# Layer 0's feed-forward gate vector summed on VectorE, GpSimd and ScalarE during the latent heads, and the third head pair's split one step a job

## The chip, the cores and the metric

The kernel runs on one core of a Trainium2 chip. A core has TensorE (matrix products, called PE in the profile; its weight loads are PEld), VectorE (DVE), ScalarE (ACT), GpSimd (POOL) and SyncE (SP, which here only issues DMAs). Each engine executes its own instructions in order and waits for the others by semaphores. The metric is the device time of one execution in microseconds (us), the median of several runs.

## What is computed

Two transformer layers over 512 latent tokens and 256 context tokens, 1024 features, all in float32. Each layer is modulated by six vectors per stream, made from a conditioning vector; the sixth, `g_f`, is the gate of the feed-forward part. Cut to what matters:

```python
for l in range(DEPTH):
    sh_a, sc_a, g_a, sh_f, sc_f, g_f = jnp.split(silu_c @ mod_w[l] + mod_b[l], 6, axis=-1)
    csh_a, csc_a, cg_a, csh_f, csc_f, cg_f = jnp.split(silu_cc @ mod_w[l] + mod_b[l], 6, axis=-1)
    a_lat, a_ctx = modulate(h_lat, sh_a, sc_a), modulate(h_ctx, csh_a, csc_a)
    ...                          # l = 0: latent heads and 2-D neighbourhood heads; l = 1: sliding window heads
    h_lat = h_lat + g_a * o_lat
    h_lat = h_lat + g_f * swiglu(modulate(h_lat, sh_f, sc_f), ffn_w_gate_up[l], ffn_w_down[l])
    if l == 0:                   # the same for the context stream, with csh_a ... cg_f
        ...
return rms_norm(h_lat, final_norm)
```

## The kernel before

The activations lie transposed, features on the 128 partitions and tokens along the free dimension, in eight tiles of 128 features. Products of full precision are made of three products of split operands: a value is cast to a high part on ScalarE and the rest is subtracted on VectorE (`split`, `parts`, `load_w`). A planner orders the instructions of each engine: it simulates the engines with its own costs and takes, of what is ready, what the program emitted first. `shifted(n)` makes what is emitted under it n places less urgent. Some stretches of the feed-forward part have a fixed order on TensorE.

Layer 0 runs in these stages, with the times of the profiled execution:

- To about 185: the input projections (`projections`, 94 steps).
- About 185 to 263: the neighbourhood heads, four pairs of heads, `na_jobs`. A pair is three jobs: the context queries, then the queries of blocks 0 and 1, then of 2 and 3. A job makes scores on TensorE, row maxima on VectorE (`take`, L546, the bias added), exponentials on ScalarE (`exps`, L542), transposes on TensorE (L483), their copies to SBUF on VectorE and ScalarE (L474, L475) and weighted sums on TensorE (L536). `attend` runs the front half of one job beside the back half of the job ahead of it, in the order of the letters of `PATTERN` (f for the front, b for the back, s for one step of side work).
- About 263 to 400: the latent heads, eight heads of two jobs, `mla_jobs`, built in the same way. Two heads ahead, `latent_operands` splits operands on ScalarE and GpSimd and copies rows by DMA on the SP queue.
- About 400 to 465: the output projection. Then the feed-forward part, `ffn`, 22 columns of 128: the first directly (`first_pairs`), the others as `Pair`s.

Side work comes from two sources. Generators that are put in the queue by `beside` advance by `step`; the number of steps a job is `STEPS`, for the four pairs of the neighbourhood heads `STEPS[0]`. One of them is `split_pair(p)`, which splits the queries (first step) and the keys (second step) of the third and fourth pair; the engine of the keys' high cast is chosen by `RK` (0: ScalarE, 2: VectorE), at L744, and the rest is subtracted on VectorE at L735.

The other source is `all_mods`, which makes the modulation vectors in the order of their need, one unit for each `next`: for layer 0 the components 2, 4, 3, 5, then those of layer 1. `bg(n)` takes n units. A component named in `PE_MODS` is made by `mods_pe`, four units: a unit loads four tiles of 256 KB on the SP queue, multiplies them on TensorE against `cond_col` (L191, 16 instructions in four column groups of 32), copies the result on ScalarE (L193), sums the groups by four small products with `pick` (L195) and adds the bias on VectorE (L199). Any other component of layer 0 is made by `mod_tile` from rows of `mod_w`, eight tiles of 512 KB in two halves, two units a tile. The first unit loads both halves and sums their products with the latent stream's conditioning vector on VectorE (L241, L245). The second multiplies the halves by the context stream's vector on GpSimd (L258), sums them on ScalarE (L259) and adds the two sums and the bias on VectorE (L261, L262). So components 2 and 3 are 16 units each, and 4 and 5, in `PE_MODS`, 4 each. Layer 1's tiles are loaded by GpSimd's queue (L212) into the tags rope0 and nb and summed on VectorE alone (L219).

In the projections `bg` takes 0.43 units a step from the ninth step on, 37 in all: components 2, 4 and 3 (36 units) and the first unit of component 5. In the heads it takes none, since the rates `BG[0]` are 0. In the feed-forward part the pairs 1 and 2 take two units each: the other three units of component 5 and the first tile of layer 1. Component 5 is used for the first time by `down0`, behind the fourth column.

## Time and profile before

| | us |
|---|---|
| median of 3 runs | 1573.08 |
| lowest and highest run | 1572.73 and 1574.07 |
| the profiled execution | 1573.01 |
| its span, from the first to the last instruction | 1571.2 |
| TensorE busy in the span | 1524.4 |
| VectorE busy | 1180.6 |
| ScalarE busy | 804.4 |
| GpSimd busy | 282.3 |
| mean granted TensorE clock | 0.992 |

Times within the execution are us from the start of the span. A row of the timeline gives start, length, engine, line, operation and operands, with the idle time ahead of it and what ended it in brackets. A row of the waits gives who waited for whom, the total in us and the number of times. Matmuls are pipelined, so that a matmul's length in the timeline is more than its share of TensorE's time; the distance from one start to the next, or the chain of waits, gives that share.

### The profile page before, as it was taken

How to read it: one execution, taken by the hardware profiler on the slowest of the kernel's cores; microseconds unless marked ns; L12 is line 12 of the kernel's file. 1: busy time of each engine (PE TensorE's matmuls, PEld its weight loads, DVE VectorE, ACT ScalarE, POOL GpSimd, SP SyncE). 2: the span in 40 equal slices, each digit the busy share in tenths (PEclk: the TensorE clock that was granted, in tenths of full speed). 3: DMA queues.
4: the chain of work that ended last, by engine and by line, in shares of the span. 5: the costliest groups of instructions: out<-in, count | busy, mean ns of one | idle time of the engine just before them, and what ended most of it. 6: DMA issues, size and time to landing. Idle time of an engine off the chain costs nothing.

```text
span 1571.2 us, 26600 instructions
## 1 busy us (share of the span) xinstructions
PE 1524.4 (97%) x9942; PEld 1355.7 (86%) x9942; DVE 1180.6 (75%) x2351; ACT 804.4 (51%) x1638; POOL 282.3 (18%) x316
## 2 busy tenths in 40 slices
PE   6999889999999999999999999999999999999998
PEld 4787767887998999999999999877789998899997
DVE  5494878657588588895877776888877778688686
ACT  5354587777376234242433345557866445354453
POOL 0173724233010010111112110382002000000000
PEclk9999999999999999999999999999999999999999
DMA  9457242102462465656566665130016133233232
GB/s 343 153 170 235 77 132 76 44 11 95 164 224 88 148 207 174 224 156 241 179 214 245 205 242 194 40 117 32 1 29 187 45 103 130 89 100 124 86 101 88
DMA packets 82129, 216.63 MB, mean 138 GB/s; under 512 B 10832, under 2 KB 18896, under 8 KB 82000
## 3 DMA queue, kind: packets, MB, share of 16 engines
q1 hardware_dynamic: 66640, 163.02, 32.4%
q0 software_dynamic: 13056, 48.77, 9.1%
q10 hardware_dynamic: 2304, 3.15, 0.5%
q8 instruction: 78, 1.28, 0.3%
q14 instruction: 51, 0.42, 0.1%
HBM read 187.10 MB, written 23.07 MB: 134 GB/s over the span
## 4 chain that ended last, share of the span: by engine, by line
PE 74%; DVE 6%; issue 4%; DMA 3%; ACT 2%; POOL 0%; DVEq 0%; POOLq 0%; ACTq 0%; SPq 0%
PE pso L536 5%; PE pss L1408 4%; PE pss L1406 4%; PE pss L1407 4%; PE pss L324 3%; PE pss L325 3%; PE psd L324 3%; PE pss L326 3%; PE psd L1408 3%; PE psd L325 3%; PE psd L1406 3%; PE psd L326 3%; PE psd L1407 3%; PE pss L768 3%; PE pst L483 2%
## 5 line engine op out<-in xcount | busy, mean ns | idle before, releaser
L311 ACT CAST wh<-wr 128x512 fp32r<-128x512 f32 (+2 forms) x139 | 105.9, 776 | 197.4 <-DMA wr<-in_w_dn_dram 39.9
L312 DVE TENSOR_TENSOR wl<-wr,wh 128x512 fp32r<-128x512 f32 (+2 forms) x136 | 127.5, 944 | 71.2 <-ACT wh L311 70.6
L542 ACT ACTIVATE p<-p,sm 128x512 f32<-128x512 f32 (+3 forms) x144 | 105.1, 730 | 34.0 <-DVE sm L546 33.3
L1408 PE MATMUL pss<-b,wl 128*128 128x384 f32 (+1 forms) x302 | 93.8, 311 | 1.9 <-DVE wl L1394 1.9
L1406 PE MATMUL pss<-b,wh 128*128 128x384 f32 (+1 forms) x302 | 93.6, 310 | 0.0
L1407 PE MATMUL pss<-b,wh 128*128 128x384 f32 (+1 forms) x302 | 93.5, 310 | 0.0
L536 PE MATMUL pso<-ph,b 128*64 128x256 f32 (+1 forms) x400 | 78.3, 354 | 2.3 <-DVE ph L474 2.1
L1406 PE MATMUL psd<-b,wh 128*128 128x384 f32 (+1 forms) x256 | 79.8, 312 | 0.6 <-ACT p L1456 0.6
L1407 PE MATMUL psd<-b,wh 128*128 128x384 f32 (+1 forms) x256 | 79.8, 312 | 0.0
L1408 PE MATMUL psd<-b,wl 128*128 128x384 f32 (+1 forms) x256 | 79.2, 311 | 0.0
L325 PE MATMUL psd<-b,wh 128*128 128x512 f32 (+3 forms) x224 | 78.4, 350 | 0.0
L536 PE MATMUL pso<-pl,b 128*64 128x256 f32 (+1 forms) x400 | 77.7, 353 | 0.2 <-ACT pl L475 0.2
L768 PE MATMUL pss<-st,st 128*128 128x512 f32 (+2 forms) x264 | 69.8, 379 | 7.8 <-DVE sm L546 7.6
L324 PE MATMUL pss<-st,wh 128*128 128x256 f32 (+2 forms) x226 | 75.5, 334 | 0.6 <-ACT st L1393 0.6
L326 PE MATMUL pss<-st,wl 128*128 128x256 f32 (+2 forms) x226 | 75.4, 334 | 0.0
L324 PE MATMUL psd<-b,wh 128*128 128x512 f32 (+3 forms) x208 | 74.9, 360 | 0.1
L326 PE MATMUL psd<-b,wl 128*128 128x512 f32 (+3 forms) x208 | 73.4, 354 | 0.0
L325 PE MATMUL pss<-b,wh 128*128 128x256 f32 (+3 forms) x223 | 70.5, 318 | 0.0
L1393 ACT CAST wh<-ph 128x512 fp32r<-128x512 f32 x80 | 46.4, 620 | 33.4 <-DVE ph L1428 14.3
L1393 ACT CAST wh<-pl 128x512 fp32r<-128x512 f32 x80 | 45.9, 619 | 30.0 <-PE psd L1407 12.2
L1393 ACT CAST wh<-wr 128x1024 fp32r<-128x1024 f32 x40 | 42.0, 1050 | 37.0 <-PE pst L325 10.1
L483 PE MATMUL pst<-ident_r,p 128*128 128x128 f32 x346 | 58.2, 277 | 1.7 <-DVE ph L474 0.6
(615 smaller groups left out, 5315.5 us busy)
## 6 DMA issues: line engine op xcount, KB each, us to landing
wr<-in_w_gu_dram SPq DMA_DIRECT2D x88, 512.0 KB, 4.1
wr<-in_w_out_dram SPq DMA_DIRECT2D x32, 512.0 KB, 3.5
wr<-in_w_dn_dram SPq DMA_DIRECT2D x64, 256.0 KB, 2.8
p<-home SPq DMA_DIRECT2D x40, 384.0 KB, 5.0
home<-p POOLq DMA_DIRECT2D x40, 384.0 KB, 5.2
nb<-in_mod_w_dram POOLq DMA_DIRECT2D x48, 256.0 KB, 3.9
rope<-in_mod_w_dram POOLq DMA_DIRECT2D x24, 512.0 KB, 4.1
wr<-in_w_in_dram SPq DMA_DIRECT2D x21, 512.0 KB, 4.9
```

The source lines that it names most:

```text
L311: S.copy(h, r)
L312: (G if eng else V).tensor_tensor(lo, r, f(h), op=ALU.subtract)
L324: PE.matmul(o, wh[:, k], mh[:, c], start=first and k == 0, stop=False)
L325: PE.matmul(o, wh[:, k], ml[:, c], start=False, stop=False)
L326: PE.matmul(o, wl[:, k], mh[:, c], start=False, stop=last and k == n - 1)
L536: ins = PE.matmul(o[64 * i : 64 * i + 64, c], v(kt), t, start=n == 0, stop=n == len(moving[i]) - 1)
L542: S.activation(p[:, c], p[:, c], AF.Exp, bias=nm, scale=-1.0, accum_out=dn)
L768: PE.matmul(o, x, k, start=i == 0, stop=i == 1)
L1393: S.copy(h, t)
L1406: PE.matmul(o, wh, xh, start=first and k == 0, stop=False, skip_group_check=not first)
L1407: PE.matmul(o, wh, xl, start=False, stop=False, skip_group_check=not first)
L1408: PE.matmul(o, wl, xh, start=False, stop=k == 3, skip_group_check=not first)
```

## The change

Component 5 of layer 0 leaves `PE_MODS`, so it is made by `mod_tile` in 16 units instead of 4. `EARLY` limits the units in the projections to 36, the rate of the latent heads' `BG[0][4]` becomes 1 unit a job, and there are 16 such jobs; pair 1 takes no unit in the feed-forward part and pair 2 takes one. The halves of component 5's tiles lie in the tag nb, of two buffers, instead of ph and pl. Apart from this, `RK[0]` goes from 2 to 0 and `STEPS[0][0]` from 2 to 1: the third pair's split advances by one step a job in the first pair's three jobs, and the high cast of its keys is made by ScalarE.

```diff
-PE_MODS = ((0, 1), (0, 0), (0, 4), (0, 5))
+PE_MODS = ((0, 1), (0, 0), (0, 4))
...
+EARLY = 36
...
-RK, RQ, RL, SQ = (2, 0), (0, 0), (0, 0), 1
+RK, RQ, RL, SQ = (0, 0), (0, 0), (0, 0), 1
...
-BG = ((0, 0, 0, 0, 0), (2, 3), (0, 0), (0, 0))
+BG = ((0, 0, 0, 0, 1), (2, 3), (0, 0), (0, 0))
...
-STEPS = ((2, 3, 4, 4), 5, 3)
+STEPS = ((1, 3, 4, 4), 5, 3)
...
-        if dense[0]:
+        if dense[0] or comp == 5:
             rs, ws = [], []
             for i in range(2):
-                w, c = T(("ph", "pl")[i], [P, 512]), slice(512 * i, 512 * i + 512)
+                w, c = T("nb" if comp == 5 else ("ph", "pl")[i], [P, 512]), slice(512 * i, 512 * i + 512)
...
-    i = 0
+    i, left = 0, EARLY
     for _ in projections():
         i += 1
         if i > 8:
-            bg(int(i * DBG) - int(i * DBG - DBG))
+            n = min(left, int(i * DBG) - int(i * DBG - DBG))
+            left -= n
+            bg(n)
...
-                    if l == 0 and j < 3:
-                        bg(2)
+                    if l == 0 and j == 2:
+                        bg(1)
```

## The prediction

> **What bounds the kernel now.** I read the page first, then the busy time by stage (the columns are window; length, busy us and instruction count of each engine, granted clock, DMA share, GB/s), because the share of the whole run hides that the three stages the change touches have three different limits.
>
> ```profile
> span 1571.2 us, 26600 instructions
> PE 1524.4 (97%) x9942; PEld 1355.7 (86%) x9942; DVE 1180.6 (75%) x2351; ACT 804.4 (51%) x1638; POOL 282.3 (18%) x316
> ...
> 185.00:263.00 78.00, 66.33 (x454) 49.12 (x452) 63.59 (x139) 58.96 (x139) 30.93 (x21) 0.91 0.36 104
> 263.00:400.00 137.00, 135.64 (x1018) 109.30 (x1015) 90.31 (x252) 98.52 (x223) 47.54 (x37) 1.00 0.21 69
> ...
> 465.00:497.00 32.00, 31.12 (x191) 26.84 (x191) 31.97 (x62) 22.17 (x40) 0.00 (x0) 1.00 0.28 92
> 497.00:515.00 18.00, 18.00 (x111) 16.50 (x110) 12.11 (x23) 8.14 (x16) 0.54 (x1) 1.00 0.39 120
> ```
>
> 185 to 263 is the neighbourhood heads: TensorE stands still for 11.7 of 78 us, VectorE is 82% busy and the granted clock is 0.91. 263 to 400 is the latent heads: TensorE is idle for 1.4 of 137 us, VectorE 66% and ScalarE 72% busy. 465 to 515 is the start of layer 0's feed-forward part: TensorE is full, but until 497 VectorE is full as well.
>
> **The change part by part.** There are five edits with three effects.
>
> First, TensorE loses the four units of component 5 (the feed-forward gate). Three ran in the feed-forward part. The chain of waits shows one run of eight of their matmuls between its neighbours; two views of those two lines alone give the busy time of all three units.
>
> ```profile
> 474.29 0.18 PE pst L1406
> 474.47 0.57 PE pss L191 x8
> 475.04 0.38 PE pst L1525
> 475.42 0.17 PE pst L1526
> ...
> ACT p L1495 <- PE pst L1529: 3.4, 1, 3.4
> ...
> 465.00:515.00 50.00, 4.85 (x48) 1.29 (x48) 1.00 0.32 102
> ...
> 465.00:515.00 50.00, 1.61 (x12) 1.65 (x12) 1.00 0.32 102
> ```
>
> A run of eight costs 0.57, and the matmul behind it 0.38 instead of 0.18, so 0.77 us in all. Busy time alone gives 4.85 + 1.61 = 6.5 us for 48 products (L191) and 12 small ones (L195). The 48 stand in seven runs, each with 0.2 us for the matmul behind it, which makes up to 1.4 more: 6.5 to 7.9, and I take 7.0. Of this about 4.6 us lie before 497 (five of the seven runs, eight of the twelve small products) and 2.4 after it. After 497 VectorE has a third of its time free, so the 2.4 count whole. Before 497 VectorE is busy for 31.97 of 32 us, and what TensorE gains may be lost again waiting for its results; I take two thirds, 3.1 us (bounds 0 and 4.6). Sum: **-5.5 us** (bounds -2.4 and -7.9). Twelve loads of 256 KB leave the SP queue here and four leave it ahead of 185; with DMA shares of 0.28 to 0.39 they were hidden, and I count them as nothing. The unit counts downstream stay aligned: the feed-forward part asked for four units at pairs 1 and 2 and now asks for one at pair 2, the same first tile of layer 1.
>
> Second, the start of the neighbourhood heads. Rows of TensorE, VectorE and ScalarE there, and three windows:
>
> ```profile
> 184.55 0.40 PE L326 MATMUL psd<-b,wl 128*128 128x512 f32 x1
> ...
> 185.87 0.73 PE L768 MATMUL pss<-st,st 128*128 128x256 f32 x4
> ...
> 187.75 0.71 PE L768 MATMUL pss<-st,st 128*128 128x512 f32 x2
> ...
> 191.73 1.22 PE L768 MATMUL pss<-st,st 128*128 128x256 f32 x4 [3.27 <-DVE sm L546]
> ...
> 184.60 0.87 DVE L744 CAST b<-p 64x768 fp32r<-64x768 f32 x1
> ...
> 185.57 1.07 DVE L735 TENSOR_TENSOR b<-p,b 64x768 fp32r<-64x768 f32 x1
> ...
> 186.28 0.69 ACT L436 ACTIVATE p<-psd,sm 128x512 f32<-128x512 f32 x1
> ...
> 186.67 2.06 DVE L744 CAST b<-p 64x768 fp32r<-64x768 f32 x1
> ...
> 187.24 1.28 ACT L542 ACT_TABLE_LOAD   x1
> ...
> 188.83 2.37 DVE L735 TENSOR_TENSOR b<-p,b 64x768 fp32r<-64x768 f32 x1
> ...
> 191.24 0.42 DVE L546 CUSTOM_DVE_ANT_0 p<-pss,zeros 128x256 f32<-128x256 f32 x1
> ...
> 191.71 0.51 ACT L542 ACTIVATE p<-p,sm 128x256 f32<-128x256 f32 x1 [3.18 <-DVE sm L546]
> ...
> 202.45 0.83 ACT L744 CAST st<-p 64x768 fp32r<-64x768 f32 x1
> ...
> 190.00:192.00 2.00, 0.27 (x1) 0.28 (x2) 1.97 (x6) 0.29 (x1) 1.92 (x2) 0.50 0.37 81
> 192.00:194.00 2.00, 2.00 (x8) 1.77 (x9) 1.45 (x10) 2.00 (x8) 2.00 (x3) 0.50 0.46 98
> 194.00:196.00 2.00, 2.00 (x8) 1.48 (x7) 0.70 (x2) 1.41 (x6) 1.39 (x1) 0.57 0.09 13
> ```
>
> The four VectorE rows at L744 and L735 are the key half of the third pair's split, 0.87 + 1.07 + 2.06 + 2.37 = 6.4 us. They sit in front of the first row maximum (L546 at 191.24), whose scores were done by 186.6. With one step a job the key half belongs to the second job, and its two casts go to ScalarE (RK 2 to 0; the fourth pair's same cast there takes 0.83). The first maximum can then start near 186, and the first exponential is held by ScalarE instead: the last raw copy ends at 186.97, the table load takes 1.28, so 188.3 in place of 191.7. That is -3.4 us. The fourth of the four removed units stood between 184.78 (184.55 plus the 0.23 us pitch of such matmuls) and 185.87, so 1.1 us; it only moves the scores, which are no longer what is late, so I don't add it. TensorE ran at half clock after this idle stretch, from 192 to about 195 with work to do; with the stretch gone I count half of these 3.2 us as gained, 1.6. Against it: the two subtractions (1.0 to 2.4 each) and 1.7 us of casts come back in a later job of a stage with VectorE at 82%, where lateness often shows: I give back 1.5. Sum: -3.4 - 1.6 + 1.5 = **-3.5 us** (bounds -6.1 with the 1.1 and nothing given back, and +2 if the later burst stops TensorE longer than this one did).
>
> [...]
>
> Third, the latent heads gain the gate: one unit in each of their 16 jobs, eight tiles of 512 KB. Prices come from the same code in the projections before, and from the late tiles where GpSimd doesn't compute (min/median/max ns):
>
> ```profile
> L241 DVE CUSTOM_DVE_ANT_0 p<-pl,cond,mod x16: 740/1514/2915, 82.6 to 180.1; 128x512 bf16<-128x512 f32 x16
> ...
> L219 DVE CUSTOM_DVE_ANT_0 p<-nb,cond,mod x32: 737/744/752, 574.7 to 907.7; 128x512 bf16<-128x512 f32 x32
> ...
> L262 DVE SCALAR_TENSOR_TENSOR mod<-mod,modb x16: 147/159/1237, 96.3 to 184.5; 128x1 f32<-128x1 f32 x16
> ...
> L258 POOL TENSOR_TENSOR ph<-ph,cond x16: 1270/1295/1799, 83.1 to 180.1; 128x512 f32<-128x512 f32 x16
> ...
> L259 ACT ACTIVATE ph<-ph x16: 619/632/633, 84.6 to 181.4; 128x512 f32<-128x512 f32 x16
> L259 ACT ACTIVATION_READ_ACCUMULATOR ph<-ph x16: 185/187/191, 85.1 to 182.0; 128x1 f32 x16
> ...
>   POOL ph L258: 11.6, 6
>   POOL pl L258: 8.2, 8
> ...
> L546 DVE CUSTOM_DVE_ANT_0 p<-pss,zeros,sm x24: 678/747/752, 278.5 to 379.9; 128x512 f32<-128x512 f32 x24
> ```
>
> VectorE: two sums a tile at 0.74 and three tiny operations at 0.16, 2.0 us, times 8 = 16 us (at 1.51 a sum, 28). GpSimd: 16 products at 1.3 = 21 us. ScalarE: 16 sums at 0.63 + 0.19 = 13 us, and it waits behind GpSimd's products: 19.8 us for 32 in the projections, so 10 for 16. VectorE goes to (90.3 + 16) / 137 = 78%, ScalarE to (98.5 + 13) / 137 = 81% (89% with its waits). The exponentials queue behind ScalarE's sums, the row maxima behind VectorE's, and TensorE's transposes wait for both. Bounds: nothing, if TensorE's backlog covers each burst of 1.5 us; and, going by the neighbourhood heads, where 82% of VectorE goes with 15% of TensorE idle, 78% would go with some 12%, 16 us instead of 1.4, so +15. I take **+3** (nearer the stage itself, whose jobs leave VectorE 46.7 and ScalarE 38.5 us free). The loads share SP with the latent heads' row copies; a load waits for one of two nb buffers, and what is queued behind it is needed two heads later. Late tile loads that GpSimd issued at 273 move behind the gate's; they are first read at 509.8.
>
> [...]
>
> Sum: -5.5 - 3.5 + 3 = -6.0. The profiled execution took 1573.01 (span 1571.2 and 1.8 around it), the median 1573.08; **1567.0 us**.
>
> **Rivals.** (a) *The latent heads become bound by VectorE and ScalarE.* Place: exponentials behind ScalarE's sums, which stand behind GpSimd's products. Price 15 us of TensorE idle, -9 + 15: 1579. It decides from 12 us on, where it costs more than the 9 gained and the 3 that can be told. For it: ScalarE's 19.8 us of waits above; against: GpSimd is two thirds free here. (b) *The gain is given back.* VectorE holds the feed-forward start (-2.4) and the moved key split stalls later (-2), with +3: 1571.7. For it: 31.97 of 32. Against: the longest wait between the computing engines there is ScalarE's for TensorE, the 3.4 at L1495. (c) *All hides.* -7, -6 and 0: 1560. That component 5 isn't done in time is no case: 36 units before and 16 jobs with one each end it.
>
> **How the numbers follow.** Forecast 0.50 (own range 1563 to 1569.8), c 0.12, b 0.20, a 0.18. About 0.2%, 3.1 us, is what a measurement of this kernel tells from no change. Faster is forecast and c, 0.62; same b, 0.20; slower a, 0.18. The range 1560.5 to 1576 leaves out half of c and the upper two thirds of a.
>
> **What would show it.** No L191 or L195 after 185; first L546 near 186 to 188 and no half clock around 190; L241, L258 and L259 spread over the latent heads with TensorE idle there under 5 us; feed-forward matmuls after 515 some 5 us nearer to the end of the latent heads. Wrong, if ScalarE's waits for L258 go on to exponentials and TensorE's idle in the latent stage passes 12 us.

## The result and the profile after

The changed kernel takes 1579.93 us, the median of six runs (1577.48 to 1584.20). The kernel before takes 1572.83 beside it, also in six (1568.46 to 1574.07). The ratio is 1.0055, with a 95% interval from 1.0042 to 1.0069: slower by about 7 us, where 6 us less were predicted, and outside the predicted range. The profiled execution of after is the slowest of its six (1584.2, span 1582.4), so its stages add up to 11 us rather than 7. That is why the stages below are compared over many kernels.

The page of after begins so:

```profile
span 1582.4 us, 26520 instructions
...
PE 1525.2 (96%) x9862; PEld 1357.5 (86%) x9862; DVE 1202.5 (76%) x2397; ACT 814.2 (51%) x1668; POOL 303.7 (19%) x332
```

TensorE has 80 instructions fewer and yet 0.8 us more busy time. That page can't say where this comes from, because the busy share is that of the whole run. The busy time by stage does. I cut both executions at the same events: the first score of the neighbourhood heads, the first and the last score of the latent heads, the token sums ahead of the feed-forward part and its first store. The prediction gave the two head stages as 185 to 263 and 263 to 400; cut at these events they run from 185.9 to 272.1 and, with the output projection, on to 464.1. The columns are those of the prediction (length; busy us and count of TensorE, its loads, VectorE, ScalarE, GpSimd; granted clock; DMA share; GB/s). Before, the neighbourhood heads up to the first latent score, the latent heads, the start of the feed-forward part:

```profile
185.90:272.10 86.20, 74.29 (x507) 55.44 (x504) 69.76 (x155) 65.89 (x156) 34.74 (x24) 0.92 0.37 104
...
272.10:379.00 106.90, 106.90 (x811) 86.96 (x810) 70.12 (x214) 77.26 (x179) 31.23 (x23) 1.00 0.09 26
...
464.10:546.10 82.00, 81.12 (x485) 73.57 (x485) 59.45 (x110) 39.99 (x75) 0.59 (x2) 1.00 0.39 124
```

After, the same three:

```profile
186.90:273.30 86.40, 72.82 (x502) 54.30 (x500) 67.75 (x152) 67.82 (x158) 35.39 (x26) 0.96 0.39 106
...
273.30:390.40 117.10, 110.33 (x809) 87.69 (x807) 95.54 (x271) 86.59 (x209) 52.24 (x39) 0.99 0.20 58
...
476.30:555.20 78.90, 75.45 (x426) 71.19 (x425) 58.55 (x104) 39.61 (x73) 0.54 (x1) 1.00 0.28 92
```

The reader is to see three things. The neighbourhood heads kept nothing of the split that was moved: 86.2 and 86.4 us. The start of the feed-forward part is 3.1 us shorter. And the latent heads are 10.2 us longer: TensorE, which had not stood still there, now idles for 6.8 us (117.1 less 110.33), and the same work (809 and 811 matmuls) takes 3.4 us more busy time. VectorE does 25.4 us more than before, ScalarE 9.3, GpSimd 21.0.

All stages together, from these events in the two traces: start of the heads +1.0, neighbourhood heads +0.2, latent heads and output projection +11.0 (192.0 to 203.0), start of the feed-forward part -3.1, the rest up to the last store of the residual -0.2, and from there to the end +2.3. The sum is the +11.2 by which the spans differ.

Who waits for whom in after, from 264 to 410 (waiting engine and tile, releaser; us in total, times, longest):

```profile
POOL nb L259 <- DVE mod L242: 26.2, 7, 9.4
...
ACT p L543 <- DVE sm L547: 11.7, 12, 2.6
...
PE pss L1115 <- DVE sm L547: 4.5, 5, 1.6
...
ACT nb L260 <- POOL nb L259: 2.0, 2, 1.5
...
PE pst L484 <- DVE ph L475: 1.8, 2, 1.2
```

The rows name VectorE. GpSimd waits for VectorE's sums (its products overwrite the tile that VectorE reads), and the exponentials and TensorE's next scores wait for VectorE's row maxima. The exponentials' wait is no sign of the change, for before, from 263 to 400, has almost as much of it:

```profile
ACT p L542 <- DVE sm L546: 10.0, 10, 1.9
```

New are TensorE's 4.5 us: before has no wait of TensorE for a row maximum there, and its largest total is 0.6 us, for a copy. ScalarE waits only 2.0 us for GpSimd's products, which was the place named in rival (a).

### The profile page after: what moved, and what is told of

Read it like the earlier page. It is cut to its first block, busy times and chain, and to the rows that moved or that the text cites. A ratio compares the mean times of both kernels' runs of the same rounds, so it can differ in the third digit from the quotient of the medians.

```text
span 1582.4 us, 26520 instructions
## 1 busy us (share of the span) xinstructions
PE 1525.2 (96%) x9862; PEld 1357.5 (86%) x9862; DVE 1202.5 (76%) x2397; ACT 814.2 (51%) x1668; POOL 303.7 (19%) x332
## 3 DMA queue, kind: packets, MB, share of 16 engines
q8 instruction: 77, 1.26, 0.3%
## 4 chain that ended last, share of the span: by engine, by line
PE 84%; DVE 8%; DMA 3%; ACT 2%; issue 1%; SPq 0%; DVEq 0%; ACTq 0%
PE pss L1411 5%; PE pss L1409 5%; PE pss L1410 5%; PE pso L537 5%; PE psd L325 4%; PE psd L326 4%; PE psd L327 4%; PE pss L325 4%; PE pss L326 4%; PE pss L327 4%; PE pst L1411 3%; PE pst L1409 3%; PE pst L1410 3%; PE pst L325 3%; PE pst L326 3%; PE pst L327 3%
## 5 line engine op out<-in xcount | busy, mean ns | idle before, releaser
L312 ACT CAST wh<-wr 128x512 fp32r<-128x512 f32 (+2 forms) x139 | 105.9, 776 | 198.3 <-PE psd L326 38.8
L1409 PE MATMUL pss<-b,wh 128*128 128x384 f32 (+1 forms) x338 | 105.2, 311 | 0.6 <-ACT p L1459 0.6
L1410 PE MATMUL pss<-b,wh 128*128 128x384 f32 (+1 forms) x338 | 105.1, 311 | 0.0
L1411 PE MATMUL pss<-b,wl 128*128 128x384 f32 (+1 forms) x338 | 104.4, 312 | 0.5 <-DVE wl L1397 0.5
L326 PE MATMUL psd<-b,wh 128*128 128x512 f32 (+3 forms) x240 | 83.5, 348 | 0.0
L1411 PE MATMUL pst<-b,wl 128*128 128x384 f32 (+1 forms) x248 | 79.0, 319 | 2.0 <-DVE wl L1397 2.0
L1409 PE MATMUL pst<-b,wh 128*128 128x384 f32 (+1 forms) x248 | 78.7, 317 | 0.0
L1410 PE MATMUL pst<-b,wh 128*128 128x384 f32 (+1 forms) x248 | 78.6, 317 | 0.0
L325 PE MATMUL psd<-b,wh 128*128 128x512 f32 (+3 forms) x200 | 73.3, 366 | 0.3 <-ACT pl L476 0.3
L327 PE MATMUL pss<-st,wl 128*128 128x512 f32 (+2 forms) x192 | 65.5, 341 | 0.0
L325 PE MATMUL pss<-st,wh 128*128 128x512 f32 (+2 forms) x192 | 65.3, 340 | 0.0
L1409 PEld LDWEIGHTS pss<-b,wh 128*128 128x128 f32 x338 | 63.7, 189 | 1.1 <-ACT p L1459 0.9
L1411 PEld LDWEIGHTS pss<-b,wl 128*128 128x128 f32 x338 | 63.6, 189 | 0.7 <-DVE wl L1397 0.7
L1410 PEld LDWEIGHTS pss<-b,wh 128*128 128x128 f32 x338 | 63.6, 188 | 0.2
```

The source lines that it names most:

```text
L312: S.copy(h, r)
L325: PE.matmul(o, wh[:, k], mh[:, c], start=first and k == 0, stop=False)
L326: PE.matmul(o, wh[:, k], ml[:, c], start=False, stop=False)
L327: PE.matmul(o, wl[:, k], mh[:, c], start=False, stop=last and k == n - 1)
L1409: PE.matmul(o, wh, xh, start=first and k == 0, stop=False, skip_group_check=not first)
L1410: PE.matmul(o, wh, xl, start=False, stop=False, skip_group_check=not first)
```

## The experiments

Three theories stood at the start. (1) VectorE's added work holds up the row maxima, alone or (1b) because GpSimd stretches it. (2) ScalarE's sums, behind GpSimd's products, hold up the exponentials: rival (a). (3) The moved split does the damage later, or (4) the planner's other order does it. All were timed in five rounds beside the kernel before. In the profiled executions I compare two lengths: the neighbourhood heads (first score to the first latent score; before 86.2) and the latent heads with the output projection (first latent score to the token sums; before 192.0). Both are differences of starts rounded to 0.1 us.

| run | us | ratio, 95% interval | neighbourhood heads | latent heads and output projection |
|---|---|---|---|---|
| split_alone | 1572.38 | 1.0008 [0.9999, 1.0017] | 87.0 | 192.4 |
| gate_alone | 1580.56 | 1.0059 [1.0046, 1.0072] | 86.2 | 202.9 |
| gate_left_out | 1569.99 | 0.9992 [0.9983, 1.0001] | 86.5 | 192.4 |
| vector_half | 1571.32 | 1.0003 [0.9994, 1.0012] | 85.3 | 195.2 |
| context_half | 1571.20 | 0.9998 [0.9989, 1.0007] | 87.2 | 195.7 |
| all_vector | 1581.02 | 1.0059 [1.0046, 1.0072] | 84.5 | 204.7 |
| no_vector | 1569.39 | 0.9993 [0.9982, 1.0005] | 85.8 | 194.1 |
| low_priority | 1578.30 | 1.0044 [1.0030, 1.0057] | 86.3 | 200.3 |
| before_copies | 1573.33 | 1.0010 [1.0001, 1.0019] | 87.1 | 193.5 |
| after_copies | 1577.85 | 1.0043 [1.0031, 1.0056] | 85.8 | 199.8 |
| low_priority_copies | 1576.13 | 1.0034 [1.0022, 1.0046] | 87.3 | 198.2 |
| no_vector_copies | 1573.75 | 1.0014 [1.0005, 1.0023] | 86.2 | 198.3 |
| no_vector_ffn | 1575.46 | 1.0026 [1.0017, 1.0035] | 84.7 | 194.1 |
| before_nb3 | 1586.87 | 1.0105 [1.0090, 1.0119] | 81.9 | 194.6 |
| split_nb3 | 1585.54 | 1.0107 [1.0087, 1.0127] | 81.9 | 194.3 |
| no_vector_nb3 | 1587.82 | 1.0112 [1.0099, 1.0125] | 84.4 | 206.1 |
| before_nb3_p7 | 1569.73 | 0.9992 [0.9982, 1.0003] | 80.6 | 192.5 |
| split_nb3_p7 | 1571.91 | 1.0011 [1.0001, 1.0021] | 86.7 | 192.4 |

### Which part costs: the split alone, the gate alone, and the gate's work left out

split_alone is the kernel before with two edits, gate_alone is after with them undone:

```diff
-RK, RQ, RL, SQ = (2, 0), (0, 0), (0, 0), 1
+RK, RQ, RL, SQ = (0, 0), (0, 0), (0, 0), 1
-STEPS = ((2, 3, 4, 4), 5, 3)
+STEPS = ((1, 3, 4, 4), 5, 3)
```

> The kernel before, with the third pair's split alone changed (one step a job, the keys' high cast on ScalarE). Theory 1 (the loss of the change is VectorE's sums in the latent heads) and theory 2 (it is ScalarE's sums behind GpSimd's products): the split costs nothing and brings up to the 3.5 us predicted, 1569 to 1573; the first exponential about 3 us sooner after the projections' end. Theory 3 (the moved split stalls later and carries the loss): 1576 to 1580.

> The kernel after with the third pair's split as before, so the gate's move alone. Theories 1 and 2: 1578 to 1583, TensorE's idle time in the latent heads 8 us or more. Theory 3: 1568 to 1571, below the kernel before, since only the products saved in the feed-forward part are left.

gate_left_out is after with every vector of layer 0's component 5 set to zero, its loads and sums left out:

```diff
+        if comp == 5:
+            if m == 0:
+                for v in vecs:
+                    G.memset(MOD[l, comp, v], 0.0)
+            for v in vecs:
+                MOD[l, comp, v, m] = ts[v]
+                yield
+            return
```

> The kernel after, leaving out the gate: component 5 of layer 0 is set to zero by two writes, with no loads and no sums; nothing of it stands in the latent heads. Theories 1 and 2: the latent heads go back to some 1.4 us of TensorE idle and the time to 1566 to 1570 (the 3 us that the feed-forward start gained stay). Theory 3, and theory 4 (the planner's other order of everything behind is the loss, whatever work the gate needs): 1575 or more.

The split makes no difference (1.0008, the interval holds 1), and the gate alone is as slow as the whole change (1.0059). Theory 3 falls. Without the gate's work the latent heads are back at their old length:

```profile
273.70:380.50 106.80, 106.80 (x811) 86.88 (x809) 70.13 (x214) 77.16 (x179) 31.20 (x23) 1.00 0.09 26
```

That row of gate_left_out is the row of before to 0.1 us, with the split and the other settings of after in place. So it is the gate's work that costs, not what else the change reorders, and theory 4 falls. It also shows the ceiling of the idea: with the gate computed nowhere the kernel reads 0.9992, 1.3 us, and the interval still touches 1. So even a gate that hides wholly could, in this form of the change, have brought little more than a measurement can tell.

### Which engine: one stream at a time, and each stream on another engine

vector_half computes only the latent stream's gate (VectorE) and sets the context stream's to zero. context_half computes only the context stream's (GpSimd and ScalarE) and sets the latent's to zero. all_vector computes both on VectorE. no_vector computes both on GpSimd and ScalarE. The core of two of these edits, first that of all_vector, then that of no_vector (context_half only leaves out VectorE's sums):

```diff
-                by_dve = TURN1[tile[0] % len(TURN1)] if tile[0] < MANY else 0
+                by_dve = 1 if comp == 5 else TURN1[tile[0] % len(TURN1)] if tile[0] < MANY else 0
...
+                if comp == 5:
+                    q = T("p", [P, 512])
+                    rs.append(T("part", [P, 1]))
+                    G.tensor_tensor(q, w, cond[:, 0, c], op=ALU.mult)
+                    S.activation(q, q, AF.Identity, accum_out=rs[i])
```

> The kernel after, leaving out the context stream's gate (set to zero): only VectorE's sums of the latent stream and the loads stay in the latent heads, nothing on GpSimd and ScalarE. Theory 1: VectorE's own 16 sums at 0.74 cost about half of the loss, 1572 to 1576, and the sums are no longer stretched. Theory 2: as with the gate left out, 1566 to 1570.

> The kernel after, leaving out the latent stream's gate (set to zero): GpSimd's 16 products, ScalarE's 16 sums and 16 operations of one column on VectorE stay in the latent heads, VectorE's 16 sums go. From the first to the last score of the latent heads it was 106.9 us before, 117.1 after, 109.8 with VectorE's sums alone. Theory 2 (ScalarE's sums behind GpSimd's products hold the exponentials): 114 us or more, time 1576 or more. Theory 1b (the loss is contention: GpSimd's products stretch VectorE's sums, and VectorE's row maxima stand behind them): 107 to 110 us, 1568 to 1572.

> The kernel after with both streams' gates summed on VectorE (32 sums of 0.7 us, nothing on GpSimd or ScalarE). VectorE's own work doubles to about 26 us. Theory 1b: twice the cost of the half alone and no contention, 111 to 114 us of latent heads, 1571 to 1575, better than after. Theory 1 (VectorE's load as such): with 26 us beside after's 16 it is as slow as after or slower, 117 us or more, 1579 or more. Theory 2: at most vector_half, 110 us, 1570 to 1572.

> The kernel after with both streams' gates made by GpSimd (32 products of 1.3 us) and summed on ScalarE (32 sums of 0.82), none on VectorE but the operations of one column. Theory 2: worse than after, 120 us or more of latent heads, 1583 or more. Theory 1b: no sums of two SBUF operands are left to be stretched, 108 to 112 us, 1569 to 1574.

The latent heads, from the first to the last score. gate_alone:

```profile
272.20:389.40 117.20, 110.38 (x810) 87.65 (x808) 95.63 (x271) 86.66 (x209) 52.30 (x39) 0.99 0.19 58
```

vector_half:

```profile
269.90:379.70 109.80, 108.39 (x810) 87.01 (x809) 86.28 (x254) 76.84 (x178) 32.14 (x24) 1.00 0.21 62
```

context_half:

```profile
271.70:381.60 109.90, 108.24 (x810) 88.06 (x809) 77.35 (x230) 86.73 (x210) 51.84 (x39) 0.98 0.21 62
```

all_vector:

```profile
271.50:389.50 118.00, 111.61 (x811) 87.89 (x810) 102.81 (x293) 78.08 (x179) 33.59 (x23) 0.99 0.20 58
```

no_vector:

```profile
271.00:379.50 108.50, 108.45 (x811) 87.55 (x810) 84.76 (x246) 95.00 (x243) 72.29 (x55) 1.00 0.21 63
```

Read the third busy number (VectorE) beside the length. With 95 to 103 us of VectorE the stage takes 117 to 118; with 77 to 86 it takes 108.5 to 110. The fourth and fifth do not order the lengths: no_vector has the busiest ScalarE (95.0) and GpSimd (72.3) of all and the shortest stage. Theory 2 falls by that run. all_vector has none of the gate's products on GpSimd (33.6 us, 2.4 more than before) and is as slow as after, so these products are not needed for the loss. Theory 1b does not fall by it in its wider sense: the stage has 31 us of GpSimd of its own, and they are in all_vector too. What stands is VectorE's work. It is not a straight line: a half costs 3 us either way, both together 10. Nor is it the load alone: context_half has 9 us less of VectorE than vector_half and is as long.

### GpSimd's part in it

The same rows are to be had for single instructions. VectorE's groups of the gate in after, from 270 to 392 (busy us, mean ns | idle before), and in vector_half, where GpSimd multiplies nothing for the gate:

```profile
L242 DVE CUSTOM_DVE_ANT_0 p<-nb,cond,mod 128x512 bf16<-128x512 f32 x8 | 10.2, 1276 | 0.3
L242 DVE CUSTOM_DVE_ANT_0 p<-nb,cond 128x512 bf16<-128x512 f32 x8 | 8.3, 1038 | 4.5 <-PE pst L484 2.3 <-PE pst L454 2.2
L246 DVE SCALAR_TENSOR_TENSOR mod<-mod,modb 128x1 f32<-128x1 f32 x8 | 5.0, 630 | 0.0
L262 DVE TENSOR_TENSOR mod<-part,part 128x1 f32<-128x1 f32 x8 | 4.1, 513 | 2.9 <-ACT nb L260 2.9
```

```profile
L242 DVE CUSTOM_DVE_ANT_0 p<-nb,cond 128x512 bf16<-128x512 f32 x8 | 9.2, 1155 | 5.6 <-PE pst L490 3.5 <-DMA nb<-in_mod_w_dram 2.1
L242 DVE CUSTOM_DVE_ANT_0 p<-nb,cond,mod 128x512 bf16<-128x512 f32 x8 | 8.3, 1036 | 0.3
...
L246 DVE SCALAR_TENSOR_TENSOR mod<-mod,modb 128x1 f32<-128x1 f32 x8 | 1.2, 150 | 0.0
```

The sums take 18.5 us in after and 17.5 in vector_half, so GpSimd's products add little to them. Both are some 1.5 times the 0.74 us a sum on which the prediction was built, and in both GpSimd has work of the stage's own: it is busy for 32.14 us in vector_half, 31.23 in before and 52.24 in after. The timelines of VectorE and GpSimd in after sort the 16 sums: five have no GpSimd instruction beside them and take 686 to 734 ns; eleven have one and take 693 to 1931, 1366 on average. What differs is L246, one element a partition: 150 ns on average in vector_half, 630 in after, where seven of the eight have a GpSimd instruction beside them. The timeline shows one such case, VectorE first, then GpSimd:

```profile
275.22 1.36 DVE L242 CUSTOM_DVE_ANT_0 p<-nb,cond,mod 128x512 bf16<-128x512 f32 x1
...
277.10 2.02 DVE L246 SCALAR_TENSOR_TENSOR mod<-mod,modb 128x1 f32<-128x1 f32 x1
279.04 0.41 DVE L547 CUSTOM_DVE_ANT_0 p<-pss,zeros 128x256 f32<-128x256 f32 x1
...
276.60 2.50 POOL L259 TENSOR_TENSOR nb<-nb,cond 128x512 f32<-128x512 f32 x2
```

GpSimd's pair of products lasts from 276.60 to 279.10. The little VectorE instruction starts inside it, at 277.10, and ends where the pair ends, at 279.12. The row maximum queued behind it comes 1.9 us late. TensorE's row of the timeline, then two windows of 3.41 us:

```profile
279.52 0.50 PE L1115 MATMUL pss<-st,st 96*128 96x512 f32 x1 [1.62 <-DVE sm L547]
```

```profile
277.41:280.82 3.41, 1.79 (x11) 1.06 (x11) 3.41 (x5) 1.32 (x4) 1.68 (x2) 1.00 0.38 143
280.82:284.23 3.41, 3.41 (x14) 2.23 (x10) 3.08 (x12) 1.96 (x7) 0.00 (x0) 0.50 0.33 88
```

TensorE pays twice: it stands still for 1.62 us behind that row maximum, and 1.3 us later it works for 3.41 us at a granted clock of 0.50, which is some 1.7 us more than at full clock, an estimate. The prediction had a stretched price for the sums alone (1.51 us, from the projections); the trace of after shows that the 128x1 instructions are stretched more, in proportion: L246 from 146 to 2016 ns, the sums from 686 to 1931.

It need not be the gate's own products. In all_vector a sum, 686 ns at the shortest, runs beside GpSimd's splitting of the stage's operands, VectorE first:

```profile
363.77 2.22 DVE L242 CUSTOM_DVE_ANT_0 p<-nb,cond 128x512 bf16<-128x512 f32 x1
...
363.61 1.83 POOL L1106 TENSOR_TENSOR st<-b,st 64x768 fp32r<-64x768 f32 x1 [5.99 <-ACT st L1105]
```

Behind that sum stands a copy, and TensorE waits 1.78 us for it, up to 366.66. The standstills of TensorE of more than 1 us are three in after (up to 279.52, 360.72 and 368.21, 4.2 of its 6.8 us of idle time), two in all_vector and one in context_half, and ahead of each VectorE has an instruction of the gate that GpSimd stretched. In context_half it is two of one element, of lines that take 0.15 us at the shortest and 1.26 and 1.74 at the longest, with TensorE idle for 1.66 us up to 302.07. Stretching alone does not stop TensorE: vector_half has a sum of 2.26 us at 329.13 and no standstill over 0.7. No run took GpSimd's own work out of the stage, so what VectorE's load costs without it isn't shown.

### Order and load: the units as filler, and the copies moved

low_priority makes the gate's units less urgent for the planner. after_copies leaves them where they are and moves 15 copies, most of them of transposed exponentials, from VectorE to ScalarE. before_copies is the control, low_priority_copies does both:

```diff
-             bg(int(len_jobs[0] * units) - int((len_jobs[0] - 1) * units))
+             with shifted(lower[0]):
+                 bg(int(len_jobs[0] * units) - int((len_jobs[0] - 1) * units))
...
-COPY = ("vva", "vvva", "vva")
+COPY = ("vva", "va", "vva")
```

> The kernel after with the gate's units emitted 150 places less urgent, as side work is, so that the planner puts row maxima, copies and exponentials first wherever they are ready. Theories 1 and 1b (the sums stand ahead of the row maxima): 108 to 112 us of latent heads, 1569 to 1574, with as much GpSimd work as after. If the order doesn't matter and the load does: 115 to 118 us, 1577 to 1581.

> After, with the copies of the latent heads' transposed exponentials spread over VectorE and ScalarE by halves ("va") in place of three quarters and one quarter ("vvva"): about 16 copies, some 11 us, leave VectorE's stretch of the latent heads for ScalarE; the gate's sums stay where they are. If the length of the latent heads follows VectorE's busy time: VectorE falls from 95.5 to 84-86 us there, the latent heads last 108-110.5 us in place of 117.1, and the time is 1569.5-1572 us. If the sums themselves, by their place in VectorE's order or by being stretched beside GpSimd, hold up the row maxima whatever VectorE's load is: the latent heads stay at 115-118 us and the time at 1577-1581.

> The control for the run with the copies moved: the kernel before with the same spread of copies and no gate sums on the other engines. The stretch of the latent heads is TensorE's there (106.9 of 106.9 us busy), so both theories expect 106.5-107.5 us and a time of 1570-1573. A gain here of over 3 us would mean that the copies are worth something of their own, and the run beside it says less about the sums.

> After with both: the gate's units planned as filler (the earlier run with that alone: 114.5 us of latent heads) and the copies of the latent heads by halves (the earlier run with that alone: 113.1 us). If the loss is VectorE's load plus a start with VectorE held beside GpSimd's first products, each run took one of the two away and together they leave 108-110.5 us, 1570-1573.5. If the place of the sums in VectorE's order costs by itself, 112-114 us and 1575-1578.

The latent heads of low_priority, after_copies and low_priority_copies:

```profile
271.60:386.10 114.50, 108.44 (x810) 86.67 (x808) 94.72 (x271) 86.40 (x209) 52.31 (x39) 1.00 0.20 59
```

```profile
270.90:384.00 113.10, 109.72 (x810) 88.26 (x809) 88.22 (x258) 91.77 (x223) 53.13 (x39) 0.98 0.20 60
```

```profile
272.30:383.20 110.90, 107.97 (x810) 87.24 (x809) 87.31 (x258) 91.45 (x223) 53.04 (x39) 1.00 0.20 61
```

Both theories missed for after_copies: 113.1 us lies between 108 to 110.5 and 115 to 118. The 114.5 us of low_priority lie between its two as well; its time is that of the second. Taking VectorE from 95.5 to 88.2 us gave back 4.0 of the 10.2. A part of the other 6 is the held start. The first 24 us of the latent heads in before, after, after_copies and low_priority:

```profile
272.10:296.10 24.00, 24.00 (x189) 19.80 (x187) 15.20 (x45) 16.96 (x40) 10.79 (x10) 1.00 0.23 66
```

```profile
273.30:297.30 24.00, 22.20 (x164) 17.94 (x164) 18.56 (x51) 16.96 (x42) 11.35 (x9) 0.93 0.30 88
```

```profile
270.90:294.90 24.00, 22.22 (x165) 17.91 (x165) 18.62 (x51) 16.94 (x42) 11.31 (x9) 0.93 0.29 89
```

```profile
271.60:295.60 24.00, 22.66 (x177) 18.47 (x176) 19.14 (x55) 18.07 (x45) 13.47 (x12) 1.00 0.31 90
```

After and after_copies begin alike: 25 and 24 matmuls behind before, some 3 us at before's 7.9 a us, with a clock of 0.93. low_priority is 12 behind, 1.5 us, at a clock of 1.00. It avoids half of that start, keeps VectorE's full load (94.7 us), and gave back 2.6 us. Both edits together gave back 6.2, and 110.9 us is near the 108 to 110.5 of the load theory.

The time did not follow: 1576.1 where 1570 to 1573.5 were expected. The control says part of why. The moved copies cost the kernel before 1.8 us by themselves (1573.33 against 1571.57 of the kernel before beside it), behind the last score, outside the stretch shown. ScalarE's casts end later there, GpSimd's subtractions follow them, and TensorE waits 1.4 us for one (L1168), where before has no such wait. By the longer measure, which holds that tail, the loss against its own control falls from 11.0 (after) to 6.3 (after_copies) and 4.7 (low_priority_copies). Of the 4.7, 1.7 are a half-clock spell behind the last score, 0.50 from 388.4 to 391.8.

So two parts are shown, VectorE's load (beside GpSimd's own work) and VectorE held beside GpSimd at the start; some 4 us of loss remain with VectorE at 87 us, and what holds them isn't separated.

> Both streams of the gate on GpSimd and ScalarE, and the copies of the transposed exponentials by halves: VectorE falls from 84.8 to about 74 us in the latent heads, ScalarE rises from 95.0 to about 104. If only VectorE's load costs time there, the latent heads last 107-108.5 us and the time is 1568-1570. If ScalarE near its full load costs as VectorE did: 112-118 us and 1573-1579.

no_vector_copies was to find out if ScalarE has the same edge. VectorE fell to 75.0 us and ScalarE rose to 99.7 of 109.0. The stretch of scores stayed at 109.0 (107 to 108.5 expected), but the token sums came 4.2 us later than in no_vector (198.3 against 194.1), and 1573.75 us is the lower end of the other theory. Of the 4.2 us, 3.4 are half clock: no_vector_copies has 0.50 from 385.0 to 391.8, and no_vector has no such spell. ScalarE near its full load seems to cost too, behind the last score; one profile each does not show it.

### The start of the feed-forward part

> Both streams of the gate on GpSimd and ScalarE as in the earlier run, and beside that the subtractions of layer 0's operand splits in front of the feed-forward part on GpSimd in place of VectorE. The stretch from the token sums to the first store of the feed-forward part gained 3.1 us with the gate gone from TensorE where 5.5 were predicted. If VectorE, which is busy without a gap there, holds the rest: 76-77 us in place of 79.0 and a time of 1566-1568. If TensorE's chain or the loads hold it: 78.5-79.5 us and 1569-1571. If GpSimd's slower subtractions come last: over 79.5 us and over 1571.

Here the subtractions of layer 0's operand splits moved from VectorE to GpSimd (an argument `eng=G` to `several`). From the token sums to the first store:

```profile
463.00:548.60 85.60, 77.39 (x426) 73.90 (x426) 60.74 (x100) 39.88 (x73) 11.73 (x6) 0.94 0.27 85
```

85.6 us instead of 79.0: the third case. TensorE's one long wait there, 6.3 us, is for a subtraction on VectorE (L1405). VectorE first waits 1.7 us for GpSimd's subtractions (ahead of 484.30), and then its own are stretched beside them (up to 2326 ns, 679 at the shortest). It does not tell whether VectorE held the rest of the gain, because those 1.7 us and the stretched subtractions cover any answer.

### Why the moved split kept nothing

The lead was there. In split_alone the first exponential starts at 187.85, ahead of before's 191.71 by 3.2 us more than the heads start earlier (185.2 and 185.9). The exponentials follow it; the 29th and the 31st of the stage, before and then split_alone:

```profile
237.15 0.71 ACT L542 ACTIVATE p<-p,sm 128x512 f32<-128x512 f32 x1
...
241.66 0.72 ACT L542 ACTIVATE wr<-wr,sm 128x512 f32<-128x512 f32 x1 [1.40 <-DVE sm L546]
```

```profile
233.64 0.72 ACT L542 ACTIVATE p<-p,sm 128x512 f32<-128x512 f32 x1 [1.01 <-DVE sm L546]
...
241.29 0.72 ACT L542 ACTIVATE wr<-wr,sm 128x512 f32<-128x512 f32 x1 [3.07 <-DVE sm L546]
```

Less the 0.7 us of the earlier start, the lead is still 2.8 us at the first and gone (-0.3) at the second; in between it had gone up and down (0.5 to 4.3). Two things differ on the way. The half-clock spells do: before has 0.50 from 188.9 to 195.7 and from 223.0 to 229.8, split_alone none at the start but from 219.3 to 229.5 and from 239.8 to 243.2. Both come to 13.6 us. And the chain of waits of split_alone has pieces of another kind, which before's has not there:

```profile
187.85 1.10 ACT p L542 x4
...
195.05 2.99 DMA nb<-in_nb_dram
...
207.61 3.52 DMA nb<-in_nb_dram
```

These are loads of the neighbourhood bias. Each head needs two tiles of it and there are two buffers, so a load waits until the row maxima of an earlier head are done. The theory was that these loads took the lead back, although the lead was still 3.7 us at the exponential of 211.89, behind the last of them. A third buffer was to show it, paid for first with buffers of the transposed exponentials and then, as those are used by the projections too, with one of the exponentials (the second added line, the runs with p7):

```diff
-BUFS = dict(b=24, part=4, st=12, wr=3, wh=3, wl=3, p=8, ph=4, pl=4, sm=10, nb=2)
+BUFS = dict(b=24, part=4, st=12, wr=3, wh=3, wl=3, p=8, ph=3, pl=3, sm=10, nb=3)
+BUFS = dict(b=24, part=4, st=12, wr=3, wh=3, wl=3, p=7, ph=4, pl=4, sm=10, nb=3)
```

> The split alone, with three buffers for the rows of the neighbourhood bias in place of two, paid for by three in place of four for each half of the transposed exponentials. If the bias's loads, whose buffers the earlier row maxima hold, took back what the split gained: the chain of waits has no or less than 4 us of these loads between 186 and 246 us (9.5 in the run with the split alone), the stretch from the first score of the neighbourhood heads to the first of the latent heads is 83-85 us in place of 87.0, and the time is 1566.5-1570. If something else follows it (ScalarE, the second split's pieces): 86-87.5 us and 1570-1573.

> Control: the kernel before with the same buffers. Its chain of waits had none of the bias's loads on it, so 86-86.5 us for that stretch and 1570-1573.5; over 1574 would mean that the smaller buffers of the transposed exponentials cost by themselves.

> Both streams of the gate on GpSimd and ScalarE, the split moved, and three buffers for the bias (the run without the third: 1569.39 us, 85.8 us for that stretch). If the loads took back the split's gain: 83-84.5 us and 1566-1568.5. If not: 85.5-87 us and 1569-1572.

The three runs reach the heads 8.6 to 9.7 us later and are 14 to 16 us slower; they only say that the neighbourhood heads are then 81.9 us long without the split moved, and 81.9 and 84.4 with it. Why the latent heads of no_vector_nb3 take 206.1 is open.

> The split alone with three buffers for the bias, paid for by seven in place of eight buffers of the exponentials. If the bias's loads took back the split's gain: 83-85 us from the first score of the neighbourhood heads to the first of the latent heads, at least 2 us less than in the control of this call. If another limit follows the start: within 1 us of the control.

> Control: the kernel before with these buffers. If the bias's loads matter only where the split is moved: 86-86.5 us for that stretch. If a third buffer helps the stage in itself, as the 81.9 us of the last two runs would say: 82-84 us. If seven buffers of exponentials are too few: over 87 us.

Here the heads start in time. before_nb3_p7, then split_nb3_p7, from the first score of the neighbourhood heads to the first of the latent heads:

```profile
185.60:266.20 80.60, 71.24 (x514) 55.74 (x511) 65.51 (x155) 65.43 (x158) 34.07 (x25) 0.94 0.39 111
```

```profile
187.10:273.80 86.70, 76.04 (x515) 57.05 (x511) 64.80 (x154) 67.93 (x160) 34.70 (x25) 0.90 0.36 103
```

The theory falls. With the third buffer no load of the bias is left in the chain or the waits of this stage in either run. Yet the stage with the split moved is still 86.7 us, while the one where the split stayed in front gained 5.6. Both do the same work (515 and 514 matmuls), and TensorE's busy time differs by 4.8 us, most of it by the granted clock, 0.94 and 0.90. So the stage comes out 5 us shorter or longer by how its pieces fall together, and a lead at its head does not decide it. What does is open.

Nor did the 5.6 us reach the median: before_nb3_p7 reads 0.9992, and the interval holds 1. Single executions of one kernel differ by some 7 us here (1566.80 to 1574.05 for before_nb3_p7), and one profile each can't say whether the 5.6 is in every one. No version tried is faster than the kernel before by more than the measurement can tell.

## Why the prediction was wrong

**The feed-forward part, -5.5 predicted, -3.1 measured.** The sign and the mechanism held, and every version without these products has the same length (78.8 to 79.4 us with the old buffers and the subtractions on VectorE, 81.9 to 82.2 with the products); the term was a little too large at both ends. TensorE's busy time fell by 5.7 us (81.12 to 75.45), not 7.0. Of that, 2.6 came back as idle time (82.00 - 81.12 = 0.9 before, 78.90 - 75.45 = 3.5 after). The window of after that lies as far behind its token sums as the prediction's 465 to 497 before shows where:

```profile
477.20:509.20 32.00, 29.59 (x164) 27.43 (x163) 32.00 (x58) 22.67 (x40) 0.00 (x0) 1.00 0.17 58
```

VectorE is busy for all of it, and TensorE idles for 2.4 us, 1.5 more than the 0.9 before. So the 1.5 us given up for that window (4.6 cut to 3.1) came out to the tenth; that two thirds would be kept was a choice, so this is luck. The 2.4 behind it, counted whole, lost 1.0, and 1.3 of the 7.0 was never there.

**The start of the neighbourhood heads, -3.5 predicted, nothing measured.** The first step was right in its order: in after the last raw copy, the table load and the first exponential follow each other without a gap, as the chain of waits of after shows.

```profile
188.39 0.69 ACT p L437
189.09 1.28 ACT L543
190.39 0.61 ACT p L543 x2
```

In time it brought less: the projections' last matmul starts 2.1 us later than before in this execution (186.66 and 184.55), the raw copy with it, so the first exponential is 1.3 us ahead of before's 191.71, or 2.3 counted from the start of the stage, and not 3.4. In split_alone, where the raw copy comes earlier, it is 3.2.

The steps that failed are the 1.5 us given back and the half-clock term. That the half clock goes with the idle stretch, as that term took it, no run shows: in before the clock was 0.50 from 188.90 on, when the stretch that ended at 191.73 had lasted 0.4 us. The prediction took a lead at the head of the stage for a gain of the stage. split_alone shows it lost by 56 us into the stage, and its stage 0.8 us longer than before. The half clock only moved there: the mean clock of the stage is 0.92 in before, as shown, and 0.92 in split_alone:

```profile
185.20:272.20 87.00, 75.36 (x508) 56.01 (x505) 67.55 (x154) 66.77 (x158) 32.51 (x24) 0.92 0.38 103
```

So the 1.6 us of that term were not won there. In after they were, as busy time, and did not help: its mean clock is 0.96, TensorE's busy time in the stage is 1.5 us less (72.82 and 74.29), and its idle time 1.7 us more (13.6 and 11.9). The bound of +2 held.

**The latent heads, +3 predicted, +10.2 measured (+11.0 with the output projection).** This is the step that turned the sign, in two places. First, VectorE's work was mis-sized: 16 us were taken, with 28 as what the same code had cost in the projections. The four groups shown come to 27.6 us; with the accumulator reads (1.3) and the last little operation (1.2) the gate took 30.1. The sums were priced at 0.74 from tiles without GpSimd, though the stage has 31 to 52 us of GpSimd, and the tiny operations at 0.16, though the row quoted for one of them already had a longest of 1237 ns. Without GpSimd the price would have been right: at the 0.70 and 0.15 us that sums and little operations take in after where no GpSimd instruction is beside them, 16 and 24 of them make 15 us, an estimate. The other half of the 30 is time beside GpSimd. Second, what such work costs was read too low. The estimate by the neighbourhood heads, where VectorE is 82% busy and TensorE 15% idle, gave up to +15. The value taken, +3, leaned on the spare time in VectorE's mean job. At 95.5 of 117.1 us, 82%, the loss is 10; at 78 to 79% it is 2 to 3 in vector_half and no_vector, but 4.0 and 6.2 in low_priority_copies and after_copies, so the share alone does not give the price. TensorE's idle time, 6.8 us, stayed under the 12 by which the prediction would have been called wrong; 3.4 us more went into matmuls that ran longer, 1.7 of it by the half-clock spell at 280.82, which an idle test can't see.

**The rivals.** Rival (a), that VectorE and ScalarE bind the latent heads, is what happened in its outcome: 1579 was its price and 1579.93 came. Its place was wrong. It had ScalarE behind GpSimd's products; the runs show VectorE, and a version with all of it on ScalarE and GpSimd (no_vector) loses 2 us there instead of 11. Rival (b), the gain given back, is nearer on both gains (-2.4 for -3.1, and -2 for nothing), and misses the loss. Rival (c) is what gate_left_out bounds: even with no gate at all the time was 1570, so 1560 was never to be had.

**The totals.** Terms of -3.1, +0.2 and +11.0 make +8.1 against the +7.1 of the medians; the profiled execution has 3.3 us more at its two ends.

## What to carry to other kernels

An engine that is not the bound has room only as far as its bursts are covered. Here 78 to 79% of VectorE's time cost 2 to 6 us in a stage of 107 by the order of its work, and 82 to 83% cost 8 to 10, so ask what the nearest stage of the same kernel loses at that load, and price added work by the same code beside the same neighbours: here it came to 30.1 us, where 15 is the estimate without GpSimd beside it. Where the work can go to any of three engines, put it on those that no waiting row names. Before pricing a move, ask what the time would be if the moved work vanished: that run bounds the gain of the move, and here it was 1.3 us.

## What the runs showed of the hardware that was not expected

In after a VectorE instruction of one element a partition, both operands in SBUF, stood until the GpSimd products beside it were done (277.10 to 279.12, beside products that end at 279.10). The rows of two such lines in after (min/median/max ns, first and last start):

```profile
L246 DVE SCALAR_TENSOR_TENSOR mod<-mod,modb x8: 146/278/2016, 277.1 to 382.1; 128x1 f32<-128x1 f32 x8
```

```profile
L262 DVE TENSOR_TENSOR mod<-part,part x8: 142/158/2852, 283.8 to 384.2; 128x1 f32<-128x1 f32 x8
```

The longest are 14 and 20 times the shortest. The row maxima of 128x512, with one operand in PSUM, take 672 to 751 ns in the 19 cases of the stage that have a GpSimd instruction beside them and 672 to 752 in the 16 that have none, and the gate's products on GpSimd are not slowed (1262 to 1299 ns, 1282 on average). So in these cases the one that is stretched is VectorE's instruction with its operands in SBUF, and the row maximum queued behind the one at 277.10 came 1.9 us late. GpSimd was stretched too: its subtraction at 395.43 in after (L1171) takes 1.73 us, 0.72 at the shortest, beside a subtraction of VectorE that began 0.9 us ahead of it.

The half clock, too, was not expected in this stage. In after TensorE stood still for 1.62 us ahead of its row at 279.52, and the clock from 280.82 to 284.23 was 0.50. The length of a standstill does not tell by itself where a spell comes. In all_vector TensorE stood still for 1.79 us up to 358.93, and the clock stayed at 1.00; it stood still for 1.78 us up to 366.66, and the clock was 0.50 from 368.36 to 371.77. Apart from the one at each trace's end, the spells of before begin at 21.64, 188.90 and 223.03 and those of after at 192.08, 226.21, 280.82, 864.50 and 1069.30; each lasts 3.41 or 6.83 us, and within a trace the starts are whole multiples of 3.413 us apart. Nor does TensorE's work in the 3.41 us ahead sort them. In after it was 1.04, 1.03 and 1.79 us ahead of the spells at 192.08, 226.21 and 280.82, and 2.08 and 2.12 from 359.33 and from 366.16, with no spell behind; in before it was 2.30 us ahead of the spell at 188.90. What sets a spell off isn't shown, and no run was made to test it.
